# A two-layer hybrid mixer and expert kernel: the first layer's S5 matrices made ahead on GpSimd during SSD, queries stacked over 128 partitions, and parameter steps given a rank

## The chip, the cores and the metric

The kernel runs on one core of a Trainium2 chip. The metric is the device time of one execution in microseconds (us); smaller is better. Its engines are named as in the profile: PE (matrix products), PEld (its weight loads), DVE (VectorE), ACT (ScalarE), POOL (GpSimd), SP (the engine that issues most DMAs). Every engine runs its own instructions in the order in which they stand in its program; an instruction that waits holds up all behind it on that engine.

## What is computed

Two layers, each a token mixer and a mixture of experts, on 512 latent tokens and 256 context tokens of width 1024, in float32. Cut to what matters here:

```
h = modulate(rmsnorm(x), shift, scale)            # norm
proj = h @ w_in                                   # split into the branches' inputs
ya = softmax(q k^T) v        # attention: 8 query heads of 64, 2 key/value heads
yb = ssd_mixer(...)          # conv, then two directions of a chunked scan, 6 chunks of 128 tokens
yc = s5_mixer(u, lambda, step, B, C)  # 24 groups of 16 channels, 64 complex states, two directions
yd = bg * conv(cg * hh)      # gated short convolution
x  = x + g * ((sum of sigmoid(gate_i) * (y_i @ w_br_i)) @ w_out)     # merge
x  = x + g2 * expert_choice_ffn(...)              # 16 experts, gate/up/down of 1024 x 1024
```

S5 needs matrices that depend on the parameters alone and not on the tokens: powers of the complex step `exp(lambda*step)`, combined with B and C into blocks for eight tokens at a time. For each c of 0 to 5 (four groups) they are T (two parts of 128x384), B (two of 128x512, then transposed on PE), C (two of 128x640) and a block KK of products of B and C. A complex product (`cmul`) is six elementwise operations: four products, a difference and a sum.

## The kernel before

Layer 0's stages in the order of the time line, read from the trace (us from the span's start): norm to about 55; SSD 60 to 320, of which convolution and z to 170, states to 180 and the six chunks from 180; the S5 input projection 320 to 390 with the parameter preparation beside it; the S5 loop 390 to 560 and its output to 600; attention 600 to 840; the rest of the filler (below) 840 to 918; merge to 1120; the experts (MoE0) to 1795. Layer 1 repeats this without the context's outputs, up to 2600, and its experts end the program at 3126.

**Two kinds of work.** `ssd`, `s5` and `attention` are written out one after the other in `branches` with `filling` off; their weights go through the tiles `raw`, `cwH` and `cwL`. Then, with `filling` on, come `shortconv`, `gate` and the later columns of `mods`: the filler. It is independent of the branches, and a scheduler, which knows program order as priority, puts its matmuls (`psmm<-hH,fwH` and its two siblings, lines 99 to 101; `psmm<-fr,cpad`, L195, for `mods`) where it sees a gap on PE. Filler weights pass through three buffers each of `fr` (the raw 128x1024 block from DRAM), `fwH` and `fwL` (its two halves in the split precision), in the pool `st`. Gate results go to `tg` (two buffers). A product in the split precision takes three matmuls: high by high, low by high, high by low.

**SSD on the engines.** For each of six column blocks m, ACT copies the projection from PSUM to `xpad` (L662), DVE convolves, ACT takes the tanh, PE transposes, ACT copies. GpSimd clears the edges of `xpad` (L595), makes `xw` (L747, 10 of them), one of the two `S*E` products of a head pair (L811, 24) and adds the off-diagonal part to `y` (L827, 20).

**S5 matrices before.** In layer 0 they are made in the S5 loop itself, chunk c beside its use: GpSimd makes B and T (`Bx`, `Tr`: lines 990 to 995, called with `nc.gpsimd`), DVE makes C, PE transposes B (L1299) and forms KK (L1308). In layer 1 they are made ahead by the generator `s5_params`, one `next` per expert step in MoE0, on DVE, written to DRAM (`s5w`) from ACT's queue, and loaded in the loop into `mt`, 1664 KB for each c. In it one buffer, `s5T`, takes T of every c in turn, so that T of c+1 waits until c's has been written out.

**Attention before.** q and k are rotated in `R`; pairs of heads are transposed (L925) and split into `qTH`/`qTL`, with 64 partitions a head; each key head is doubled on DVE into `kd` before its transpose. `scores` forms q k^T with K=64 and the usual three matmuls for each head and each key half.

Of the kernel before, what the change touches and what calls it, by code (L numbers as in the profile page):

```python
# [45 lines left out]
_PS5 = {}  # L46
# [12 lines left out]
class Kern:  # L59
# [86 lines left out]
    def setup(self):  # L146
# [30 lines left out]
        self.s5w = {1: dr("s5w1", 6, 128, self.S5W)}  # L177
        self.s5r = {1: dr("s5r1", 128, 24)}
# [100 lines left out]
    def mixer(self, l):  # L279
# [42 lines left out]
    def norm(self, l):  # L322
        nc, L0 = self.nc, l == 0
        with self.pool("np") as np_:
# [24 lines left out]
            if L0:  # L349
                rows = []  # L350
                for q in range(5):
# [288 lines left out]
    def ssd(self):  # L640
# [12 lines left out]
        with self.pool("conv"):  # L653
            for m in (4, 5, 0, 1, 2, 3):
# [8 lines left out]
                self.vt = "a"  # L663
                cv = self.wp.tile([128, 770], F32, name="cv")
# [99 lines left out]
        with self.pool("core") as wp:  # L764
# [83 lines left out]
            for i, c in enumerate(self.tiles):  # L848
# [3 lines left out]
                y = chunk(c, *now)  # L852
                if last:
# [5 lines left out]
    def attention(self):  # L859
# [4 lines left out]
        qT = [wp.tile([128, 4, 768 - q0], F32R, name="qT" + p) for p in "HL"]  # L864
        kT = [wp.tile([128, 2, 768], F32R, name="kT" + p) for p in "HL"]
        Vt = wp.tile([128, NT, 128], F32, name="Vt")
        with self.pool("rope") as rp:
# [14 lines left out]
            for nm, m, c in (("k", 0, C_K), ("q", 0, C_Q), ("q", 1, C_Q + 256)):  # L882
# [31 lines left out]
                for o, n in (self.streams if nm == "q" else [(256, 512), (0, 256)]):  # L914
                    for g in range(2):
                        ps = self.va(n)
                        for i in range(n // 128):
                            t = o // 128 + i
                            if nm == "k":
                                kd = rp.tile([128, 2, 64], F32, name="kd", bufs=2)  # L920
                                V.tensor_copy(kd, R[:, t, g][:, None, :].to_broadcast([128, 2, 64]))
                                src = kd
                            else:
                                src = R[:, t, 2 * g:2 * g + 2]
                            nc.tensor.transpose(ps[:, i * 128:(i + 1) * 128], src.rearrange("p a c -> p (a c)"), self.ident)  # L925
                        self.split_to(*(z[:, 2 * m + g, o - q0:o - q0 + n] if nm == "q" else z[:, g, o:o + n] for z in (qT if nm == "q" else kT)), ps)
        R2 = [slice(0, 64), slice(64, 128)]

        def scores(t, hp):
# [8 lines left out]
            for i in range(np_):  # L938
                for hh in range(2):
                    q2, k2 = ([z[R2[hh], hp, tk] for z in qT], [z[R2[hh], hp // 2, i * pn:(i + 1) * pn] for z in kT])  # L940
                    self.mm3(sc[i][hh], [(*q2, *k2)])
# [57 lines left out]
    def s5_params(self, l, pool):  # L999
# [5 lines left out]
        sm = lambda nm, *s, tag=None: pool.tile([128, *(s or (24,))], F32, name="s5" + nm, tag="s5" + (tag or nm))  # L1005
        p5 = sm("p5", NPS5 - 384)
        Q.dma_start(p5, I["ps5"][l, :, 384:])
        pr = {k: p5[:, a - 384:b - 384] for k, (a, b) in _PS5.items()}

        step, mag, ang = sm("step"), sm("mag"), sm("ang")  # L1010
# [4 lines left out]
        t, sn, cn, rho = sm("t"), sm("sn"), sm("cn"), sm("rho")  # L1015
# [16 lines left out]
        x1 = sm("x1", 8, 24)  # L1032
# [12 lines left out]
        un, lo, hi = sm("un", 2, 9, 24), sm("lo", 2, 17, 24, tag="big"), sm("hi", 2, 6, 24)  # L1045
# [15 lines left out]
        for c in range(6):  # L1061
            gg = slice(4 * c, 4 * c + 4)
            T, e1 = sm("T", 2, 4, 6, 16, tag="out"), sm("e1", 4, 6, 16, tag="e1")
# [3 lines left out]
            Q.dma_start(out[c][:, 2560:], T.rearrange("p i g a b -> p (i g a b)"))  # L1067
            yield
        pw = sm("pw", 2, 9, 24, tag="un")
# [7 lines left out]
        nr, den, cr, ci = sm("nr"), sm("den"), sm("cr"), sm("ci")  # L1077
# [16 lines left out]
        PB, PC = sm("PB", 2, 8, 24), sm("PC", 2, 10, 24, tag="hi")  # L1094
# [8 lines left out]
        bb = [sm(f"bb{i}", 5, 16) for i in range(2)]  # L1103
# [3 lines left out]
        for c in range(6):  # L1107
# [4 lines left out]
            e1 = sm("e1", 4, 10, 16)  # L1112
            self.cmul(V, bb[0][:, :4], bb[1][:, :4], bc(cr), bc(ci), v3(pr["br"])[:, gg], v3(pr["bi"])[:, gg], e1[:, :, 0])
            Bx = sm("Bx", 2, 4, 8, 16, tag="big")
            ap = lambda P, n, i: P[:, i, :, gg].rearrange("p s g -> p g s")[:, :, :, None].to_broadcast([128, 4, n, 16])
            av = lambda v, n: v[:, :, None, :].to_broadcast([128, 4, n, 16])
            self.cmul(V, Bx[:, 0], Bx[:, 1], ap(PB, 8, 0), ap(PB, 8, 1), av(bb[0][:, :4], 8), av(bb[1][:, :4], 8), e1[:, :, :8])
            yield
            Bt = sm("Bt", 2, 4, 128, tag="out")
            for i in range(2):  # L1120
                ps = self.pa(512)
                for q in range(4):
                    nc.tensor.transpose(ps[:, q * 128:(q + 1) * 128], Bx[:, i, q].rearrange("p s i -> p (s i)"), self.ident)
# [3 lines left out]
            Cx = sm("Cx", 2, 4, 10, 16, tag="big")  # L1127
            self.cmul(V, Cx[:, 0], Cx[:, 1], ap(PC, 10, 0), ap(PC, 10, 1), av(cc[0][:, gg], 10), av(cc[1][:, gg], 10), e1)
            nc.scalar.mul(Cx[:, 1], Cx[:, 1], -1.0)
            for i in range(2):  # L1130
                Q.dma_start(out[c][:, 1024 + 512 * i:1536 + 512 * i].rearrange("p (g s j) -> p g (s j)", g=4, s=8),
                            Cx[:, i, :, 1:9].rearrange("p g s j -> p g (s j)"))
            yield

            KK = sm("KK", 4, 15, 16, tag="out")[:16]
            kf = [self.pa(128).rearrange("p (d j) -> p d j", d=8) for _ in range(2)]
            for d in range(2):
                r = slice(d * 64, d * 64 + 64)
# [12 lines left out]
            yield  # L1151

    def s5(self):
# [20 lines left out]
        hoisted = l == 1  # L1174
        if hoisted:
            s5d, rho = wp.tile([128, 384], F32, name="s5d"), wp.tile([128, 24], F32, name="rho")
            nc.scalar.dma_start(s5d, self.I["ps5"][l, :, :384])
            nc.scalar.dma_start(rho, self.s5r[l])
        else:
            keep = lambda nm, *s: wp.tile([128, *s], F32, name=nm)  # L1180
            bb = [keep("bbr", 25, 16), keep("bbi", 25, 16)]
            cc = keep("cc", 2, 24, 16)
            s5d = keep("s5d", 384)
            PB, PC = keep("PB", 2, 8, 24), keep("PC", 2, 10, 24)
            rho = keep("rho", 24)
            lo, hi = keep("lo", 2, 17, 24), keep("hi", 2, 6, 24)
            with self.pool("s5p") as pp:
                sm = lambda nm, *s: pp.tile([128, *(s or (24,))], F32, name=nm)
                p5 = sm("p5", NPS5 - 384)
                nc.scalar.dma_start(p5, self.I["ps5"][l, :, 384:])  # L1190
                nc.scalar.dma_start(s5d, self.I["ps5"][l, :, :384])
                pr = {k: p5[:, a - 384:b - 384] for k, (a, b) in _PS5.items()}
                V.tensor_copy(cc[:, 0], v3(pr["cr"]))
                V.tensor_copy(cc[:, 1], v3(pr["ci"]))

                step, mag, ang = sm("step"), sm("mag"), sm("ang")
                nc.scalar.activation(step, pr["ls"], AF.Exp)
                V.tensor_mul(mag, pr["lr"], step)
                nc.scalar.activation(mag, mag, AF.Exp)
                V.tensor_mul(ang, pr["li"], step)  # L1200
                t, sn, cn = sm("t"), sm("sn"), sm("cn")
                M = 12582912.0
                V.tensor_scalar(t, ang, 1.0 / (2 * np.pi), M, op0=OP.mult, op1=OP.add)
                V.tensor_scalar(t, t, M, None, op0=OP.subtract)
                V.scalar_tensor_tensor(ang, t, -6.28125, ang, op0=OP.mult, op1=OP.add)
                V.scalar_tensor_tensor(ang, t, -(2 * np.pi - 6.28125), ang, op0=OP.mult, op1=OP.add)
                V.tensor_scalar(ang, ang, 3.1415925, -3.1415925, op0=OP.min, op1=OP.max)
                nc.scalar.activation(sn, ang, AF.Sin)
                nc.scalar.activation(cn, ang, AF.Sin, scale=0.5)
                V.tensor_mul(cn, cn, cn)  # L1210
                V.tensor_scalar(cn, cn, -2.0, 1.0, op0=OP.mult, op1=OP.add)
                pw = sm("pw", 2, 9, 24)
                x1 = sm("x1", 8, 24)
                V.memset(pw[:, 0, 0], 1.0)
                V.memset(pw[:, 1, 0], 0.0)
                V.tensor_mul(pw[:, 0, 1], mag, cn)
                V.tensor_mul(pw[:, 1, 1], mag, sn)

# [587 lines left out]
```

## Time and profile before

| | |
|---|---|
| median of 3 runs | 3125.06 us (3124.32 to 3130.27) |
| the profiled execution | 3127.88 us, span 3126.0 us, mean granted clock 0.970 |
| PE busy in the span | 2857.1 us (91%) |
| DVE / ACT / POOL busy | 1615.0 (52%) / 790.0 (25%) / 444.5 (14%) us |
| layer 0 before its merge | 0 to 918 us |
| the S5 loop of layer 0, of layer 1 | 390 to 560, 2095 to 2200 us |
| layer 1's experts | 2600 to 3126 us, DMA at 409 GB/s |

The shares of the whole span hide that each stage has its own limit. PE is busy nearly all the time in layer 0 but for the first 40 us and for the S5 loop; in layer 1's experts the weights' transfer sets the pace. A view by stretch (busy time of each engine in windows) therefore tells more here than the page's totals. In that view "PEclk" is the granted clock of TensorE as a share of its upper level: 1.00 is 2.4 GHz, 0.50 would be 1.2 GHz, and values between are means over a stretch. Matmuls are pipelined, so that the mean duration of one is longer than the distance between two starts.

### The profile page before, as it was taken

How to read it: one execution, taken by the hardware profiler on the slowest of the kernel's cores; microseconds unless marked ns; L12 is line 12 of the kernel's file. 1: busy time of each engine (PE TensorE's matmuls, PEld its weight loads, DVE VectorE, ACT ScalarE, POOL GpSimd, SP SyncE). 2: the span in 40 equal slices, each digit the busy share in tenths (PEclk: the TensorE clock that was granted, in tenths of full speed). 3: DMA queues.
4: the chain of work that ended last, by engine and by line, in shares of the span. 5: the costliest groups of instructions: out<-in, count | busy, mean ns of one | idle time of the engine just before them, and what ended most of it. 6: DMA issues, size and time to landing. Idle time of an engine off the chain costs nothing. (4 is left out here: it accounts for less than half of the span.)

```text
span 3126.0 us, 47474 instructions
## 1 busy us (share of the span) xinstructions
PE 2857.1 (91%) x18866; PEld 1850.2 (59%) x18866; DVE 1615.0 (52%) x3681; ACT 790.0 (25%) x1733; POOL 444.5 (14%) x551
## 2 busy tenths in 40 slices
PE   7999878999999976999999979999999996998887
PEld 4866756787788952444444448577777884332223
DVE  5477688655326676354522264767654365232223
ACT  4253222425422210011100033321445221000001
POOL 1022265100004120000010010400000031010001
PEclk9999989999999988999999989999999998999999
DMA  7324424311247357898998663255312576999997
GB/s 234 114 67 132 141 86 126 121 48 35 98 156 226 123 204 290 346 344 330 352 372 332 235 210 98 63 167 199 98 44 80 199 265 256 409 409 409 409 409 301
DMA packets 328832, 667.18 MB, mean 213 GB/s; under 512 B 22177, under 2 KB 197537, under 8 KB 327842
## 3 DMA queue, kind: packets, MB, share of 16 engines
q1 hardware_dynamic: 297712, 610.31, 54.4%
q10 hardware_dynamic: 27378, 43.18, 3.8%
q0 software_dynamic: 3520, 10.65, 0.9%
q8 instruction: 149, 2.44, 0.3%
q14 instruction: 73, 0.60, 0.1%
HBM read 609.94 MB, written 52.56 MB: 212 GB/s over the span
## 5 line engine op out<-in xcount | busy, mean ns | idle before, releaser
L1507 PE MATMUL psa<-we,X 128*64 128x512 f32 (+1 forms) x4096 | 593.2, 492 | 49.1 <-DMA we<-in_w_exp_gate_dram 18.3
L1507 PEld LDWEIGHTS psa<-we,X 128*64 128x64 f32 (+1 forms) x4096 | 202.5, 124 | 406.3 <-issue 279.1
L99 PE MATMUL psmm<-hH,fwH 128*128 128x512 f32 x984 | 369.9, 376 | 6.8 <-DVE xpad L632 3.6
L101 PE MATMUL psmm<-hH,fwL 128*128 128x512 f32 x984 | 365.1, 371 | 0.0
L100 PE MATMUL psmm<-hL,fwH 128*128 128x512 f32 x984 | 363.9, 370 | 0.0
L1539 PE MATMUL psa<-we,hidT 128*64 128x512 f32 x992 | 243.9, 611 | 16.1 <-ACT hidT L1527 11.1
L99 PEld LDWEIGHTS psmm<-hH,fwH 128*128 128x128 f32 x984 | 188.1, 191 | 51.7 <-issue 15.3
L101 PEld LDWEIGHTS psmm<-hH,fwL 128*128 128x128 f32 x984 | 188.1, 191 | 33.0 <-issue 6.7
L100 PEld LDWEIGHTS psmm<-hL,fwH 128*128 128x128 f32 x984 | 188.3, 191 | 31.5 <-issue 6.3
L1520 ACT ACTIVATE hid<-psa 128x512 f32<-128x512 f32 (+1 forms) x48 | 25.3, 527 | 605.4 <-PE psa L1507 442.7
L115 DVE TENSOR_TENSOR fwL<-fr,fwH 128x1024 fp32r<-128x1024 f32 (+1 forms) x100 | 109.6, 1097 | 124.0 <-ACT fwH L114 113.4
L1539 PEld LDWEIGHTS psa<-we,hidT 128*64 128x64 f32 x992 | 70.9, 139 | 159.4 <-issue 121.3
L1544 DVE SCALAR_TENSOR_TENSOR y<-psa,ag,m 64x512 f32<-64x512 f32 x62 | 46.5, 749 | 224.6 <-PE psa L1539 223.9
L1498 POOL TENSOR_TENSOR X<-X,modT 128x512 f32<-128x512 f32 x40 | 41.5, 1050 | 697.2 <-DVE X L1497 694.5
L469 POOL TENSOR_TENSOR merged<-merged,tgm 128x512 f32<-128x512 f32 (+1 forms) x48 | 62.5, 1321 | 516.8 <-DMA y<-ys 274.4
L99 PE MATMUL psa<-cwH,hH 128*128 128x256 f32 (+1 forms) x432 | 122.4, 284 | 1.7 <-DVE dtv L697 1.6
L114 ACT CAST fwH<-fr 128x1024 fp32r<-128x1024 f32 (+1 forms) x100 | 89.4, 895 | 132.2 <-PE psmm L100 70.0
L101 PE MATMUL psa<-cwH,hL 128*128 128x256 f32 (+1 forms) x432 | 121.6, 282 | 0.0
L100 PE MATMUL psa<-cwL,hH 128*128 128x256 f32 (+1 forms) x432 | 121.4, 281 | 0.0
L1522 DVE TENSOR_TENSOR hid<-hid,psa 128x512 f32<-128x512 f32 (+1 forms) x48 | 28.7, 597 | 176.7 <-PE psa L1507 176.4
L1521 DVE SCALAR_TENSOR_TENSOR hid<-hid,psa 128x512 f32<-128x512 f32 (+1 forms) x48 | 28.7, 598 | 144.4 <-ACT hid L1520 144.3
L414 ACT ACTIVATE tg<-psmm 128x512 f32<-128x512 f32 x96 | 50.9, 530 | 202.1 <-PE psmm L101 202.0
(645 smaller groups left out, 5860.6 us busy)
## 6 DMA issues: line engine op xcount, KB each, us to landing
we<-in_w_exp_gate_dram SPq DMA_DIRECT2D x128, 1024.0 KB, 8.7
we<-in_w_exp_up_dram SPq DMA_DIRECT2D x128, 1024.0 KB, 13.8
we<-in_w_exp_down_dram SPq DMA_DIRECT2D x128, 1024.0 KB, 15.1
fr<-in_w_mod_dram SPq DMA_DIRECT2D x96, 512.0 KB, 6.5
fr<-in_w_in_dram SPq DMA_DIRECT2D x64, 512.0 KB, 4.2
raw<-in_w_in_dram SPq DMA_DIRECT2D x36, 512.0 KB, 4.0
gs<-tg ACTq DMA_DIRECT2D x32, 384.0 KB, 2.8
tgm<-gs SPq DMA_DIRECT2D x32, 384.0 KB, 3.3
```

Source lines behind the costliest of these rows:

```text
L99: self.nc.tensor.matmul(ps, ah, bh, start=start and i == 0, stop=False)
L100: self.nc.tensor.matmul(ps, ah, bl, start=False, stop=False)
L101: self.nc.tensor.matmul(ps, al, bh, start=False, stop=stop and i == n - 1)
L114: self.nc.scalar.copy(h, x)
L115: self.nc.vector.tensor_sub(l, x, h.bitcast(F32))
L414: nc.scalar.activation(tg[:, o:o + n], self.cm(w, m, o, n), AF.Tanh, scale=0.5)
L469: (V if i == 3 else nc.gpsimd).tensor_add(dst, dst, t)
L1498: nc.gpsimd.tensor_add(X[:, hk], X[:, hk], Bm[:, 24 + h * 4:28 + h * 4, s:s + 1].to_broadcast([128, 4, 128]))
L1507: self.lastup = nc.tensor.matmul(ps[s][j * c:(j + 1) * c], X[s][:, k, r:r + c], w(k)[:, j * n:(j + 1) * n], start=k == 0, stop=k == 7, ski ...
L1521: V.scalar_tensor_tensor(hid, hid, 1.0, g, op0=OP.add, op1=OP.mult)
L1539: nc.tensor.matmul(ps[j * c:(j + 1) * c], lh, w(k)[:, j * n:(j + 1) * n], start=k == 0, stop=k == 7, skip_group_check=True)
L1544: V.scalar_tensor_tensor(Y[s][r, nn], ps[j * c:(j + 1) * c], got[s][1][r, e:e + 1], m5[s][r, nn], op0=OP.mult, op1=OP.mult)
```

## The change

Three things are changed.

1. **Layer 0's S5 matrices are made ahead.** `s5_params(0, st)` starts before the norm, and `advance()` takes one step of it at places in the norm, the convolution, z, the states and the chunks of SSD, with its priority number raised by 600 (a later rank). What is left is drained before `s5`. All six operations of each big product of T, B and C are on GpSimd (`E`), the small ones on DVE. Results go to DRAM and come back into `mt` as in layer 1. Its scratch tiles take all three buffers of each of `fwH`, `fwL` and `fr`, and one of `tg`; C and B share the places `c0` and `c1`, and T, the transposed B and KK share `out`.
2. **Rank in MoE0.** Layer 1's steps go through `advance` too, and from expert 1 on.
3. **Queries stacked.** Each query head is doubled into `kd`, now on GpSimd with three buffers, and transposed alone; `qS` holds the high part on partitions 0 to 63 and the low part on 64 to 127. A score is then two matmuls with K=128 (`qS` by `kTH`, `qS` by `kTL`).

```diff
                 with self.psum(*MIX[l]):
+                    if l == 0:
+                        self.ahead = self.s5_params(0, st)
+                        next(self.ahead)
                     self.norm(l)
@@ norm, in the loop over q
+                    if q > 2:
+                        self.advance()
@@ branches
+            if nm == "s5":
+                for _ in self.ahead:
+                    pass
@@ ssd: convolution, z, states, chunks
                 self.vt = "a"
+                self.advance()
...
             for t in range(NT):
+                self.advance()
...
                 for i, c in enumerate(order[:-1]):
+                    self.advance()
...
                 y = chunk(c, *now)
+                for _ in range(2):
+                    self.advance()
@@ attention
-        qT = [wp.tile([128, 4, 768 - q0], F32R, name="qT" + p) for p in "HL"]
+        qS = wp.tile([128, 8, 768 - q0], F32R, name="qS")
...
+                            kd = rp.tile([128, 2, 64], F32, name="kd", bufs=3)
+                            nc.gpsimd.tensor_copy(kd, R[:, o // 128 + i, g][:, None, :].to_broadcast([128, 2, 64]))
+                            nc.tensor.transpose(ps[:, i * 128:(i + 1) * 128], kd.rearrange("p a c -> p (a c)"), self.ident)
...
+                            z = qS[:, 4 * m + g, o - q0:o - q0 + n]
+                            nc.scalar.copy(z, ps)
+                            V.tensor_sub(z[64:], ps[64:], z[64:].bitcast(F32))
...
-                    self.mm3(sc[i][hh], [(*q2, *k2)])
+                    for z in range(2):
+                        nc.tensor.matmul(sc[i][hh], qS[:, 2 * hp + hh, tk], kT[z][:, hp // 2, i * pn:(i + 1) * pn], start=z == 0, stop=z == 1)
@@ s5_params
+        E = V if l else nc.gpsimd
...
+            for i, nm in enumerate(("pa", "c0", "c1", "e1", "hi", "un", "PB", "sm", "out")):
+                tag = ("fwH", "fwL", "fr")[i // 3]
+                place[nm] = pool.tile([128, 1024], F32, name="s5" + nm, tag=tag, bufs=3)
...
-            self.cmul(V, T[:, 0], T[:, 1], h4(0), h4(1), l4(0), l4(1), e1)
+            self.cmul(E, T[0], T[1], h4(0), h4(1), l4(0), l4(1), e1)
...
+    def advance(self):
+
+        p = self.tc.cur_priority
+        self.tc.cur_priority = p + 600
+        next(self.ahead, None)
+        self.tc.cur_priority = p
@@ s5: the branch that made the matrices in the loop is gone
-                    self.cmul(nc.gpsimd, Bx[0], Bx[1], ap(PB, 8, 0), ap(PB, 8, 1), av(bb[0], 8), av(bb[1], 8), e1)
-                    self.cmul(V, Cx[0], Cx[1], ap(PC, 10, 0), ap(PC, 10, 1), av(cc[:, 0], 10), av(cc[:, 1], 10), z1)
...
-                    self.cmul(nc.gpsimd, T[0], T[1], h4(0), h4(1), l4(0), l4(1), e1[:, :, :6])
+                mt = bp.tile([128, self.S5W], F32, name="mt", bufs=2)
+                nc.sync.dma_start(mt, self.s5w[l][g0 // 4])
@@ experts, after each k
-                    if k == 1:
-                        next(self.ahead, None)
+                    if k == 1 and e:
+                        self.advance()
```

How the instructions stand, in the order of each engine's program (out<-in by tile names; xN: N alike in a row).

PE before, in the convolution of SSD, where the first filler matmul stands (the 130th row of PE's program):

```order
L100 MATMUL psb<-hL,cwH 128x256
L101 MATMUL psb<-hH,cwL 128x256
L99 MATMUL psmm<-hH,fwH 128x512
L100 MATMUL psmm<-hL,fwH 128x512
L101 MATMUL psmm<-hH,fwL 128x512
```

PE of the change, the place of the first filler matmul (the 788th row); L853 transposes y of SSD's last chunk, L1164 transposes B, L1182 is KK:

```order
L1182 MATMUL psb<-s5c_125,s5sm 32x128
L853 MATMUL psa<-cst,y 128x128 x4
L1164 MATMUL psb<-cst,s5c_124 128x128 x4
L1164 MATMUL psb<-cst,s5c_125 128x128 x4
L1182 MATMUL psb<-s5c_124,s5sm 32x128
L99 MATMUL psmm<-hH,fwH 128x512
```

No filler matmul stands between SSD's instructions any more; the steps of `s5_params` do.

POOL before, from the end of the norm into SSD:

```order
L347 TENSOR_TENSOR hL<-hf,hH 128x512
L347 TENSOR_TENSOR hL<-hf,hH 128x256
L595 MEMSET xpad 128x1 x28
L747 TENSOR_TENSOR xw<-x_tok,wdd 128x512 x10
L811 TENSOR_TENSOR S<-S,E 128x128 x4
```

POOL of the change, at the end of the norm (lines 1004 to 1009 are one complex product, here T; L350 is the norm's last `hL`, L603 the edges of `xpad`):

```order
L1009 TENSOR_TENSOR s5out<-s5out,s5e_126 128x384
L1005 TENSOR_TENSOR s5e_126<-s5hi,s5c_124 128x384
L350 TENSOR_TENSOR hL<-hf,hH 128x512
L350 TENSOR_TENSOR hL<-hf,hH 128x256
L1004 TENSOR_TENSOR s5out<-s5hi,s5c_124 128x384
L350 TENSOR_TENSOR hL<-hf,hH 128x512
L350 TENSOR_TENSOR hL<-hf,hH 128x256
L1006 TENSOR_TENSOR s5out<-s5out,s5e_126 128x384
L603 MEMSET xpad 128x1 x4
```

Thirteen T operations stand before the norm's fifth pair of `hL` and fourteen before the sixth; all 36 and B and C of c=0 to 2 stand before the last `xw`, c=3 and 4 among the chunks' `S*E` and `y`, and c=5 behind them.

ACT before, in the convolution:

```order
L662 COPY xpad<-psa 128x512
L114 CAST cwH<-raw 128x1056
L114 CAST cwH<-raw 128x4x256
L662 COPY xpad<-psa 128x256
L198 COPY row<-psmm 128x256
L667 ACTIVATE th<-cv 128x770
```

ACT of the change, in front of the copy of m=2 (L1165 copies the transposed B, L1170 negates a part of C, L1186 and L1188 copy KK, L1166, L1172 and L1190 issue writes to `s5w`):

```order
L1186 COPY s5out<-psb 16x128 x4
L1188 COPY s5out<-psb 16x112
L695 COPY x_tok<-psa 128x4x128
L695 COPY x_tok<-psa 128x2x128
L1188 COPY s5out<-psb 16x112 x3
L1190 DMA s5w_91<-s5out 16x4x128 x6
L670 COPY xpad<-psa 128x512
```

KK of c=0 stands before `xpad` of m=2, KK of c=1 before z, KK of c=2 before the first decays of the chunks. In MoE0 the order on DVE is that of before at the place where T of layer 1 is made: these operations stand between the two halves of expert 1's `hid`.

## Rows read from the trace of the kernel before

**Rows 1.** Busy time by stretch, all engines, layer 0's stages and layer 1's S5 loop.

```profile
core 0: us, PE busy (x) PEld busy (x) DVE busy (x) ACT busy (x) POOL busy (x), PEclk, DMA share, GB/s
60.00:180.00 120.00, 117.82 (x785) 98.38 (x783) 57.27 (x109) 34.13 (x63) 11.00 (x30) 1.00 0.34 99
180.00:320.00 140.00, 131.72 (x751) 93.93 (x752) 104.46 (x290) 72.55 (x204) 33.26 (x49) 1.00 0.36 109
320.00:390.00 70.00, 63.04 (x408) 51.00 (x412) 46.05 (x169) 18.12 (x31) 15.39 (x14) 0.95 0.43 138
390.00:560.00 170.00, 143.19 (x1137) 108.84 (x1124) 146.00 (x244) 43.21 (x103) 97.39 (x89) 0.89 0.34 103
560.00:918.00 358.00, 348.93 (x2369) 284.11 (x2367) 161.05 (x459) 145.52 (x361) 16.25 (x16) 0.99 0.25 81
2095.00:2200.00 105.00, 98.18 (x625) 74.28 (x624) 80.87 (x192) 21.96 (x31) 9.52 (x25) 0.98 0.50 168
```

**Rows 2.** The same for tile fwH: columns PE, PEld, DVE, ACT, clock, DMA.

```profile
60.00:320.00 260.00, 91.34 (x332) 56.09 (x333) 14.24 (x18) 12.41 (x18) 1.00 0.35 104
840.00:880.00 40.00, 36.38 (x150) 25.51 (x151) 7.35 (x6) 6.30 (x6) 1.00 0.61 212
```

**Rows 3.** The same for tile fwL: PE, PEld, DVE, clock, DMA.

```profile
60.00:320.00 260.00, 57.75 (x166) 31.28 (x166) 14.24 (x18) 1.00 0.35 104
840.00:880.00 40.00, 25.28 (x76) 14.30 (x76) 7.35 (x6) 1.00 0.61 212
```

**Rows 4.** The same for line L195 (mods) in SSD: PE, PEld, clock, DMA.

```profile
60.00:320.00 260.00, 14.18 (x160) 4.60 (x160) 1.00 0.35 104
```

**Rows 5.** The same for lines L1308 (KK), then L1299 (B transposed), around the loop.

```profile
300.00:620.00 320.00, 7.97 (x192) 4.28 (x192) 0.93 0.40 124
...
300.00:620.00 320.00, 6.44 (x48) 5.45 (x48) 0.93 0.40 124
```

**Rows 6.** Time line of POOL, norm: start, duration, instruction, idle before.

```profile
38.46 2.89 POOL L347 TENSOR_TENSOR hL<-hf,hH 128x512 fp32r<-128x512 f32 x2 [2.78 <-DVE hf L346]
...
52.23 1.97 POOL L347 TENSOR_TENSOR hL<-hf,hH 128x512 fp32r<-128x512 f32 x2 [1.35 <-DVE hf L346]
```

**Rows 7.** Busy time by stretch, tile Tr (DVE, POOL), then tile Bx (PE, PEld, POOL).

```profile
300.00:620.00 320.00, 25.13 (x48) 33.99 (x24) 0.93 0.40 124
...
300.00:620.00 320.00, 6.44 (x48) 5.45 (x48) 35.03 (x24) 0.93 0.40 124
```

**Rows 8.** POOL operations on tile e: duration ns min/median/max.

```profile
L991 POOL TENSOR_TENSOR e<-PB,bbi x6: 1102/1372/1584, 362.5 to 511.0; 128x512 f32<-128x512 f32 x6
```

**Rows 9.** Tile s5T in MoE0: operation, then idle before it and who waited.

```profile
L990 DVE TENSOR_TENSOR s5T<-s5hi,s5lo x6: 1108/1116/1118, 1170.6 to 1226.1; 128x384 f32<-128x384 f32 x6
...
  DMA s5w<-s5T: 18.6, 5
...
  ACT hid L1520: 35.7, 1
```

**Rows 10.** DMA issues of the page: tile, queue, count, KB, median us to landing.

```profile
s5w<-s5Cx ACTq DMA_DIRECT2D x12, 256.0 KB, 12.9
```

**Rows 11.** Groups of POOL operations up to 620 us: busy us, mean ns, idle before.

```profile
L827 POOL TENSOR_TENSOR y<-y,yo 128x256 f32<-128x256 f32 x20 | 18.7, 937 | 23.7 <-DVE y L816 10.2 <-DVE rs_y L126 4.8 <-DVE rs_t L125 3.0
L811 POOL TENSOR_TENSOR S<-S,E 128x128 f32<-128x128 f32 x24 | 13.5, 561 | 61.4 <-DVE S L810 59.5 <-PE psmm L101 1.2 <-DVE rs_y L136 0.6
L747 POOL TENSOR_TENSOR xw<-x_tok,wdd 128x512 f32<-128x512 f32 x10 | 11.1, 1149 | 55.4 <-DVE wdd L738 55.4
```

**Rows 12.** Time line of DVE in MoE0: one of the small parameter operations.

```profile
1170.02 0.18 DVE L991 TENSOR_TENSOR s5x<-s5hi 128x24 f32<-128x24 f32 x1
```

**Rows 13.** Time line of PE in layer 1's attention: two transposes, three score matmuls.

```profile
2286.78 0.38 PE L925 MATMUL psa<-cst,R 128*128 128x128 f32 x2
2287.09 0.44 PE L99 MATMUL psa<-kTH,qTH 64*128 64x384 f32 x1
...
2287.81 0.50 PE L101 MATMUL psmm<-hH,fwL 128*128 128x512 f32 x1
```

**Rows 14.** Groups of POOL operations in the whole span that have one input.

```profile
L1468 POOL COPY pick<-identb 16x128 bf16<-16x128 bf16 x20 | 6.2, 321 | 121.3 <-PE psmm L1470 119.7 <-PE psmm L101 1.6
```

**Rows 15.** POOL in the whole span: two-input additions of 128x128 in attention.

```profile
L908 POOL TENSOR_TENSOR R<-R,tp 128x128 f32<-128x128 f32 x4 | 2.8, 706 | 32.7 <-DVE tp L907 30.0 <-DVE rs_v L124 2.7
```

More of the change, by code (lines that the diff above doesn't have):

```diff
@@ L175, in setup @@
         self.gs = [dr(f"gs{b}", 8, 128, 768) for b in range(4)]
-        self.s5w = {1: dr("s5w1", 6, 128, self.S5W)}
-        self.s5r = {1: dr("s5r1", 128, 24)}
+        self.s5w = [dr(f"s5w{l}", 6, 128, self.S5W) for l in range(2)]
+        self.s5r = [dr(f"s5r{l}", 128, 24) for l in range(2)]
         self.hr = [[dr(f"hr{l}{s}", n, D) for s, n in enumerate((512, 256)[:2 - l])] for l in range(2)]
@@ L1004, in s5_params, with at, small, bank @@
         v3 = lambda a: a.rearrange("p (g i) -> p g i", g=24)
[L1005 to L1010, printed above, removed]
+        E = V if l else nc.gpsimd
+        place = {}
+        if l:
+            for nm, n in (("pa", 840), ("pb", 768), ("c0", 816), ("c1", 640), ("out", 1024), ("e1", 640), ("hi", 480), ("un", 432), ("PB", 384), ("sm", 616)):
+                place[nm] = pool.tile([128, n], F32, name="s5" + nm)
+        else:
+            for i, nm in enumerate(("pa", "c0", "c1", "e1", "hi", "un", "PB", "sm", "out")):
+                tag = ("fwH", "fwL", "fr")[i // 3]
+                place[nm] = pool.tile([128, 1024], F32, name="s5" + nm, tag=tag, bufs=3)
+            place["pb"] = pool.tile([128, 768], F32, name="s5pb", tag="tg", bufs=2)
+        used = [0]
+        def at(nm, *shape, o=0):
+            n = int(np.prod(shape))
+            ax = "abcd"[:len(shape)]
+            return place[nm][:, o:o + n].rearrange(f"p ({' '.join(ax)}) -> p {' '.join(ax)}", **dict(zip(ax, shape)))
+        def small(*shape):
+            shape = shape or (24,)
+            used[0] += int(np.prod(shape))
+            return at("sm", *shape, o=used[0] - int(np.prod(shape)))
+        def bank(n):
+            return self.pa(n) if l else self.va(n, "b")
+        pr = {}
+        for nm, o, n in (("pa", 384, 840), ("pb", 1224, 768)):
+            Q.dma_start(place[nm][:, :n], I["ps5"][l, :, o:o + n])
+            pr.update({k: place[nm][:, c - o:d - o] for k, (c, d) in _PS5.items() if o <= c < o + n})
+        step, mag, ang = (small() for _ in range(3))
         nc.scalar.activation(step, pr["ls"], AF.Exp)
@@ L1014, in s5_params @@
         V.tensor_mul(ang, pr["li"], step)
-        t, sn, cn, rho = sm("t"), sm("sn"), sm("cn"), sm("rho")
+        t, sn, cn, rho = (small() for _ in range(4))
         M = 12582912.0
@@ L1031, in s5_params @@
         yield
-        x1 = sm("x1", 8, 24)
+        x1 = small(8, 24)
         def powers(P, first, last):
@@ L1062, in s5_params @@
             gg = slice(4 * c, 4 * c + 4)
-            T, e1 = sm("T", 2, 4, 6, 16, tag="out"), sm("e1", 4, 6, 16, tag="e1")
+            T, e1 = [at("out", 4, 6, 16, o=i * 384) for i in range(2)], at("e1", 4, 6, 16)
             h4 = lambda i: hi[:, i, :, gg].rearrange("p a g -> p g a")[:, :, :, None].to_broadcast([128, 4, 6, 16])
             l4 = lambda i: lo[:, i, 1:17, gg].rearrange("p a g -> p g a")[:, :, None, :].to_broadcast([128, 4, 6, 16])
-            self.cmul(V, T[:, 0], T[:, 1], h4(0), h4(1), l4(0), l4(1), e1)
-            Q.dma_start(out[c][:, 2560:], T.rearrange("p i g a b -> p (i g a b)"))
+            self.cmul(E, T[0], T[1], h4(0), h4(1), l4(0), l4(1), e1)
+            Q.dma_start(out[c][:, 2560:], place["out"][:, :768])
             yield
-        pw = sm("pw", 2, 9, 24, tag="un")
+        pw = at("un", 2, 9, 24)
         V.memset(pw[:, 0, 0], 1.0)
@@ L1075, in s5_params @@
         yield
-        nr, den, cr, ci = sm("nr"), sm("den"), sm("cr"), sm("ci")
+        nr, den, cr, ci = (small() for _ in range(4))
         ni = pw[:, 1, 1]
@@ L1102, in s5_params @@
         yield
-        bb = [sm(f"bb{i}", 5, 16) for i in range(2)]
+        bb = [small(5, 16) for i in range(2)]
         for b in bb:
@@ new lines, in s5 @@
+                mt = bp.tile([128, self.S5W], F32, name="mt", bufs=2)
+                nc.sync.dma_start(mt, self.s5w[l][g0 // 4])
+                Bt = [mt[:, i * 512:i * 512 + 512].rearrange("p (q c) -> p q c", q=4) for i in range(2)]
+                Cx = [mt[:, 1024 + i * 512:1536 + i * 512].rearrange("p (q c) -> p q c", q=4) for i in range(2)]
+                T0 = mt[:, 2048:2560].rearrange("p (q c) -> p q c", q=4)
+                T = [mt[:, 2560 + i * 384:2944 + i * 384].rearrange("p (q c) -> p q c", q=4) for i in range(2)]
@@ L1341, in s5 @@
                 H = [W(f"Vr{i}", 4, 96) for i in range(2)]
[L1342 removed]
+                g1, g2 = W("g1", 4, 96), W("g2", 4, 96)
                 V.tensor_mul(H[0], T[0], pv[0])
```

189 lines of the change are left out of this document (25 added, 164 removed).

## The prediction

> **What bounds the kernel now.** I read the busy time by stretch first, since a change to one stage is worth what that stage's limit lets through; then what the filler takes in SSD, POOL's operations in the norm and the S5 loop, the waits around T in MoE0, and one stretch of attention.
>
> From 60 to 320 us PE is busy 117.82 + 131.72 of 260 us at clock 1.00 [rows 1]: SSD has no gap to speak of, because filler lies in its gaps. How much: fwH's matmuls are busy 91.34 us there and fwL's 57.75 [rows 2, 3], together 149.1; these overlap, and in 840 to 880, where there is little else, 36.38 + 25.28 = 61.7 us of them fill 40 us [rows 2, 3]. So the filler takes 149.1 x 40/61.7 = 97 us of PE in SSD; the mods matmuls another 14.18 busy [rows 4], about 10 by the same ratio. SSD's own PE work is 249.5 - 107 = 142.5 us.
>
> In the S5 loop PE is busy 143.19 of 170 us at a clock of 0.89, with DVE at 146 and POOL at 97 [rows 1]. At full clock its work is 143.19 x 0.89 = 127 us: 43 us is lost to waiting and to the clock. Layer 1's loop, with its matrices loaded, is busy 98.18 of 105 us at 0.98 [rows 1], a loss of 9. That difference is what the first part can win there. Attention is bound by PE: 348.93 of 358 us from 560 to 918 [rows 1].
>
> **Layer 0 as a sum.** Once the filler may start, PE has work to the end of the layer: whatever is left is done one after the other. So the end of the stage before the merge is T + W + L: T the time at which the filler starts, W PE's work that is left, L what is still lost. Before, it is 918.
>
> W: the work from 60 to 918 at full clock is 249.5 + 63.04 x 0.95 + 143.19 x 0.89 + 348.93 x 0.99 = 782 us [rows 1]. SSD's own 142.5 goes off, and the 8 + 6 us of KK and B transposes [rows 5], which now lie ahead of T. That leaves 625. Attention's saving takes 14 off (below): W = 611. L: 9 in the S5 loop as in layer 1, 13 elsewhere (358 - 345 from 560 on): 22. The end is T + 633, plus 4 for `kd` (below). Layer 0 breaks even at T = 281.
>
> **T, the price.** Filler weights need the buffers in which the parameters' scratch lies, and in PE's order the first filler matmul comes behind the last KK; so T is the end of the GpSimd chain of 36 operations each for T, B and C, or the end of SSD, whichever is later. The T part of the generator has a lower end and an upper end:
>
> - An operation with `Tr` as its output took 33.99/24 = 1.42 us on POOL, one with `Bx` 35.03/24 = 1.46 [rows 7]; the e products are alike. So T takes 8.5 us for a c, B 8.8, and C, with 640 for 512 elements, 10.9 (worked out from B). The fastest product of 512 took 1.10 [rows 8]: then 6.6, 6.6 and 8.3. In all 169 us, or 129.
> - T's single output buffer: in MoE0 the next T sat behind the write 18.6 us in 5 times, 3.7 us each [rows 9]. B of c+1 overwrites what C of c lies in, which ACT must negate, PE read and a DMA write; such a write landed in 12.9 us in MoE0 [rows 10], whose DMA load was higher than SSD's 0.34 to 0.36 [rows 1]. I take 5, near the lower row, and 1.2 for eight B transposes at 0.155 [rows 13].
> - The first T can start when four pairs of `hL` are done, 38.46 + 2.89, about 42 [rows 6]. Two more pairs (2 us each) lie within: the T part ends at 42 + 51 + 5 x 3.7 + 4 = 115. Each c then takes 8.8 + 10.9 + 1.2 + 5 = 25.9, six 155: 270. SSD's own POOL work, 18.7 + 13.5 + 11.1 = 43 us [rows 11], lies in between, half of it in the waits: 292, and 296 with the last KK.
> - ACT's order ties SSD to the chain: KK of c=0 stands in front of `xpad` for m=2, KK of c=2 in front of the chunks' decays. KK of c=2 is there at 115 + 3 x 25.9 = 193, with `xw` on POOL 204. The six chunks took 140 us with filler, and DVE is busy 104 of these [rows 1], some of it for filler; without, I take 104: T = 308.
>
> T = 308, then, from two ways that agree within 12 us. The end of the stage is 308 + 633 + 4 = 945, 27 us later than 918. The floor: the T part ends at 42 + 40 + 18.5 = 101 with `hL` in its waits, a c takes 6.6 + 8.3 + 1.2 + 3.7 = 19.8, KK of c=2 is there at 160, `xw` at 171, and the chunks take 100, without the filler's share of DVE (of 14.24 in SSD [rows 2]): T = 271. The ceiling: 12.9 in the place of 5 gives 33.8 for a c, KK of c=2 at 216, 227 with `xw`, chunks 104 to 140: 331 to 367.
>
> The norm: 60 small DVE operations of 0.18 us [rows 12] now stand ahead of the reciprocal root, at most 11 us, and T operations ahead of the last two `hL` pairs, which ended at 54 [rows 6]. Both delay SSD's begin; it costs nothing in the sum above, since the chain on GpSimd is later anyway, and up to 11 where it is not. PE will wait in SSD, and its granted clock will sink as it did in the S5 loop (0.89). That costs nothing while GpSimd is last; were it PE, 157 us at 0.89 would be 19 more.
>
> The Trainium skill (GPSIMD Engine Reference, Elementwise — side-by-side cycle accounting) puts a two-input float32 operation on GpSimd at 1.96 times VectorE's. The same product of 128x384 took 1.116 on DVE [rows 9], which would make 2.19 on GpSimd; POOL's rows say 1.42 on the mean [rows 7]. The measurement decides; by the page's ratio T's 24 products would take 24 x 0.77 = 18 us more, and the forecast would be 3161.
>
> **Attention.** In layer 1's attention three score matmuls took from 2287.09 to 2287.81, 0.72 us [rows 13], for two now 0.48: 0.24 less. Layer 0 has 4 tiles x 8 heads x 2 halves = 64 of 384 columns and 16 of 256, 15.4 + 2.6 us; layer 1 64, 15.4. Transposes: 24 more in layer 0, 16 in layer 1, at most 0.155 each [rows 13]: 3.7 and 2.5. So 14 and 13 us less on PE. Against it, `kd` comes from GpSimd, 60 copies and 44, in bursts between which PE has one filler matmul for three transposes. With 226 filler matmuls in 40 us [rows 2, 3] that is (3 x 0.155 + 0.18)/3 = 0.215 us for each transpose. A one-input copy of 128 elements took 0.321 on POOL, though of 16 partitions [rows 14]; a two-input addition of 128x128 0.706 [rows 15]. I take 0.32: PE loses 0.1 for some 39 and 35 transposes that are not first in a burst, 4 us in each layer. By 0.706 it would be 19 and 17, by none 0. The Trainium skill (GPSIMD Engine Reference, Engine selection) says that one-input operations run at about line rate on GpSimd; by it the 8 us would be near nothing. Layer 1 gains 13 - 4 = 9, on the path, since PE is the limit there.
>
> **Rank.** T of layer 1 still stands between the halves of expert 1's `hid`, behind which ACT waited 35.7 us [rows 9]. The order there is that of before, so I cost it at nothing; were those waits gone, 18.6 us of DVE's waiting would be the gain.
>
> **The sum.** 3127.9 + 27 - 9 = 3146 by the profiled execution, which is 2.8 above the median of the runs: 3143.
>
> **The rivals.**
>
> *SSD runs freely without the filler.* PE is no longer shared and the chain runs at POOL's fastest rows: T = 271, 37 us less, 3106. For it: 107 us of foreign work leaves SSD, and DVE is less loaded than beside POOL in the S5 loop (146 of 170). Against it: KK of c=2 must then be there by 160, with no SSD work of POOL in its way. It turns to a gain where T is below 290.
>
> *The single buffers decide.* Writes land in 12.9 us: T = 331, 3166, and up to 3202 with slow chunks. For it: B and C share their places, T, B and KK another, and ACT must issue eleven writes for a c in between its own SSD work. Against it: DMA is loaded a third only.
>
> *`kd` on GpSimd holds PE.* At 0.706 the gain of attention is eaten in both layers: 28 us more, 3171 with T = 308, 3134 with T = 271.
>
> *The rank ends the wait in MoE0.* 3124 with the rest as forecast, no change. The order speaks against it.
>
> **The numbers.** My forecast's own region (T from 296 to 330) has a chance of 0.42, 3131 to 3165. The free SSD 0.27; the buffers or `kd`, above that, 0.20; what lies about break-even, the rank among it, 0.11. No change is within 0.2%, about 6 us, T from 284 to 296. So faster 0.27, same 0.11, slower 0.62. The range for 8 in 10 goes from 3102, below the free SSD, to 3182, between the buffers' two prices.
>
> **What would show it.** Right: by stretch, PE well under full from 60 to 300 with POOL busy, and the first `psmm<-hH,fwH` at about 308; POOL's T operations from 42 to 115; ACT's `xpad` waiting for KK; the S5 loop near 105 us; merge starting at about 945; fewer PE us in attention, PE waiting there for POOL `kd` in pieces of a tenth of a us. Wrong: the first filler before 280, the chunks' first decays before 190, or a c on POOL of 20 us or less. Then the free SSD is what happened. A start after 330 with POOL idle for the writes would be the buffers.

## The result, and the profile after

The changed kernel takes 3295.14 us (median; 3293.98 to 3299.1) against 3127.07 for before on the same chip: a ratio of 1.0547, 95% interval 1.0523 to 1.0571. It is slower by 168 us. The prediction had the sign and not the size: it gave 3143, with a range up to 3182.

The page of the changed kernel: span, busy time and share by engine, and the granted clock in 40 slices.

```profile
span 3293.0 us, 47471 instructions
PE 2907.8 (88%) x18762; PEld 1882.2 (57%) x18762; DVE 1597.6 (49%) x3661; ACT 797.7 (24%) x1745; POOL 515.4 (16%) x691
PEclk9685599999999998899899998999999998899999
```

The clock sinks in slices 2 to 5, about 80 to 410 us: that is SSD. Where else time went is read from instructions that both kernels have. In both traces, tile by tile, columns count: duration ns min/median/max, first to last start; here the experts' first matmul, and the first step of a norm on `x`, layer 1's begin. Before:

```profile
L1507 PE MATMUL psa<-we,X x4096: 379/498/1114, 1143.6 to 3094.3; 128*64 128x512 f32 x99, 128*32 128x256 f32 x97
...
L333 ACT ACTIVATE junk<-x x6: 1052/1053/1057, 1807.2 to 1819.7; 128x1024 f32<-128x1024 f32 x6
```

The changed kernel:

```profile
L1417 PE MATMUL psa<-we,X x4096: 379/498/1117, 1278.9 to 3261.1; 128*64 128x512 f32 x99, 128*32 128x256 f32 x97
...
L336 ACT ACTIVATE junk<-x x6: 1052/1054/1057, 1985.8 to 1999.0; 128x1024 f32<-128x1024 f32 x6
```

Layer 0's mixer is 135 us longer (1278.9 - 1143.6), MoE0 another 43 (1985.8 - 1807.2 is 179), and layer 1 gives 12 back (167 at the end).

By stretch in the changed kernel (columns as in [rows 1]): SSD in three parts, and layer 0's S5 loop.

```profile
80.00:200.00 120.00, 68.67 (x424) 58.62 (x423) 44.66 (x71) 25.63 (x54) 66.02 (x63) 0.74 0.22 63
200.00:240.00 40.00, 30.52 (x236) 24.57 (x236) 22.46 (x49) 9.63 (x19) 16.76 (x14) 0.83 0.33 99
240.00:400.00 160.00, 99.23 (x336) 61.35 (x334) 105.33 (x262) 69.01 (x207) 74.72 (x79) 0.54 0.13 37
440.00:545.00 105.00, 97.84 (x782) 76.57 (x781) 85.25 (x201) 14.70 (x29) 11.70 (x38) 1.00 0.62 203
```

The loop gave what layer 1's showed: 105 us in the place of 170 [rows 1]. SSD lost more. PE has less to do there than before, is busy for 62% of the time from 240 to 400 us, at a granted clock of 0.54, and the filler starts only at 401 us:

```profile
L99 PE MATMUL psmm<-hH,fwH x984: 276/393/793, 401.1 to 2636.5; 128*128 128x512 f32 x131, 128*128 128x256 f32 x66
```

So T, forecast at 308, is 401. The waits say what SSD stood in. First PE's from 60 to 235 us, then POOL's from 60 to 407 (engine, line, what it waited for: us in all, times, longest); L691 transposes the convolution's output, L1182 is KK, L1164 the transposes of B, L1004 the first operation of C.

```profile
PE psa L691 <- DVE cv L684: 21.8, 2, 19.7
PE psb L1182 <- POOL s5c L1006: 14.2, 3, 5.3
PE psb L1164 <- POOL s5c L1006: 11.6, 2, 9.8
PE psb L1182 <- ACT s5c L1170: 7.5, 2, 3.8
...
POOL s5c L1004 <- PE psb L1164: 44.8, 3, 35.3
```

PE waits at KK and at the transposes for GpSimd (14.2 and 11.6 us, and 7.5 more for the part of C that ACT negates), with SSD's matmuls behind them. Its wait for `cv` is in sum no longer than without any S5 steps, where it is 24.8 us (the held run below). From 235 to 407 PE waits another 22 us at the same two places. GpSimd in turn waits for PE's transposes, which stand behind SSD's matmuls in PE's order. The longest of these waits on POOL's time line (idle before it in brackets), and all engines in that stretch:

```profile
221.29 1.57 POOL L1004 TENSOR_TENSOR s5c<-s5hi,s5pb 128x640 f32<-128x640 f32 x1 [35.33 <-PE psb L1164]
...
185.96:221.30 35.34, 35.30 (x297) 35.13 (x296) 14.12 (x44) 8.66 (x18) 0.01 (x2) 1.00 0.24 70
```

Here GpSimd stood for 35 us in front of C, for eight transposes that were sized at 1.2 us. PE did not wait in that time: it was busy for 35.30 of 35.34 us at clock 1.00, nearly all of it with SSD's own z projection. So this wait held back the S5 chain and not SSD, and the steps behind it came to lie among the chunks.

### The profile page after: what moved, and what is told of

Same layout as the page of the kernel before. It is cut to its first block, busy times and chain, and to the rows that moved or that the text cites. A ratio compares the mean times of both kernels' runs of the same rounds, so it can differ in the third digit from the quotient of the medians.

```text
span 3293.0 us, 47471 instructions
## 1 busy us (share of the span) xinstructions
PE 2907.8 (88%) x18762; PEld 1882.2 (57%) x18762; DVE 1597.6 (49%) x3661; ACT 797.7 (24%) x1745; POOL 515.4 (16%) x691
## 5 line engine op out<-in xcount | busy, mean ns | idle before, releaser
L1417 PE MATMUL psa<-we,X 128*64 128x512 f32 (+1 forms) x4096 | 610.9, 497 | 44.6 <-DMA we<-in_w_exp_gate_dram 16.3
```

The lines of the kernel that those rows point to most:

```text
L1417: self.lastup = nc.tensor.matmul(ps[s][j * c:(j + 1) * c], X[s][:, k, r:r + c], w(k)[:, j * n:(j + 1) * n], start=k == 0, stop=k == 7, ski ...
```

## The experiments

Theory: three separate causes. Layer 0's mixer is long because the filler is shut out of SSD and because S5 steps stand in line with SSD's instructions; MoE0 is long because of the rank; attention gains. Rivals are in each expectation. Each time of the kernel before was taken on the same chip as the run beside it.

**Rank undone** (in the changed kernel):

```diff
-                    if k == 1 and e:
-                        self.advance()
+                    if k == 1:
+                        next(self.ahead, None)
```

> The changed kernel with one part undone: in MoE0 layer 1's parameter steps are taken as before, from expert 0 on and without the later rank. In the changed kernel the time line stands 134 us behind before at MoE0's begin and 179 behind at its end. Theory 1 (the rank costs these 44 us, because it spreads the steps into experts where PE has nothing else to hide them): 3295 - 44 = about 3251. Theory 2 (the new layout of the scratch, in which whole places are shared, makes the steps wait): no change, 3295 within 6.

Measured: 3241.09 us (3239.94 to 3245.71), 54 less than the changed kernel. The rank, not the scratch's layout, is MoE0's loss.

**Attention alone** (the kernel before with the new `qS`, `scores` and `kd`):

> The kernel before with the attention of the change alone: stacked queries, two score matmuls, kd on GpSimd. Theory 1 (PE is the limit in both layers, kd costs little): 14 - 4 and 13 - 4 us less, 3127 - 19 = about 3108. Theory 2 (kd on GpSimd holds PE): 3127 within 6. In the changed kernel layer 1 gained 12 us between the ends of MoE0 and of its merge, which speaks for theory 1.

Measured: 3107.7 against 3124.07, a ratio of 0.9944 (0.9928 to 0.9961): 16 us, near theory 1. Its experts' first matmul, and the `kd` copies in the changed kernel (0.343 us each on the mean):

```profile
L1508 PE MATMUL psa<-we,X x4096: 378/498/1116, 1133.1 to 3075.1; 128*64 128x512 f32 x99, 128*32 128x256 f32 x97
...
L933 POOL COPY kd<-R 128x128 f32<-128x128 f32 x60 | 18.4, 343 | 19.6 <-DVE R L927 12.1 <-PE psa L934 7.3
```

**No parameter work in layer 0:**

```diff
-                        self.ahead = self.s5_params(0, st)
-                        next(self.ahead)
+                        for c in range(6):
+                            nc.sync.dma_start(self.s5w[0][c], I["w_in"][0, c * 128:c * 128 + 128, :self.S5W])
+                        nc.scalar.dma_start(self.s5r[0], I["w_in"][0, 0:128, 4000:4024])
```

> The changed kernel without any parameter work in layer 0: its S5 matrices are not made, the DRAM blocks that the loop loads are filled from w_in by seven transfers at the start. The filler's buffers are then free in SSD. It leaves out the making of layer 0's S5 matrices, and says what the hoist is worth at no price. Theory 1 (all that the hoist costs lies in SSD, and the S5 loop gives back what layer 1's loop shows): layer 0 gains 43 - 9 = 34 in the loop and 10 in attention, layer 1 gains 10, the rank costs 44: 3127 - 54 + 44 = about 3117. Theory 2 (PE has no less to do, and the idle time only moves): 3127 - 20 + 44 = about 3151.

Measured: 3122.49 against 3124.07 (ratio 0.9998, 0.9989 to 1.0008), 5 above theory 1. But its seven transfers stand ahead of the norm's loads: the convolution's first tanh starts at 94.2 us in the place of 60.3 (below), 34 us later. Where layer 0's mixer ends is read from the experts' first matmul, before the rank has any part:

```profile
L1418 PE MATMUL psa<-we,X x4096: 378/498/1117, 1108.4 to 3092.8; 128*64 128x512 f32 x99, 128*32 128x256 f32 x97
```

It comes 35 us earlier than before (1143.6) in spite of the 34; attention alone gives 10.5 of that (1133.1). So making the S5 matrices ahead, at no price, is worth about 35 + 34 - 10.5 = 59 us, more than the 34 of theory 1.

**The same with the filler's buffers held** through SSD:

```diff
+                        self.hold = [st.tile([128, 1024], F32, name=f"hold{i}", tag=("fwH", "fwL", "fr")[i // 3], bufs=3) for i in range(9)]
+                        for h in self.hold:
+                            nc.gpsimd.memset(h[:, :1], 0.0)
...
+                for h in self.hold:
+                    nc.vector.tensor_add(h[:, :1], h[:, :1], last[1][:, :1])
```

> As the run without parameter work, but nine tiles hold all buffers of fr, fwH and fwL from the norm until the last chunk of SSD is finished, so that the filler starts where it does in the changed kernel. It leaves out the making of layer 0's S5 matrices. Theory 1 (SSD was slow because its engines stood in line behind the S5 steps): SSD ends at about 300 instead of 401, and the time is about 3295 - 100 = 3195. Theory 2 (SSD is slow because PE, without filler, falls to the lower clock): SSD ends at 370 or later with a granted clock of 0.5 to 0.6 in the chunks, and the time is 3265 or more.

Measured: 3231.25 us (two runs), between the two theories. Against the run without parameter work that is 109 us for nothing but the filler's absence from SSD. Its experts' first matmul, and PE's wait for `cv` in SSD:

```profile
L1422 PE MATMUL psa<-we,X x4096: 379/498/1117, 1212.5 to 3201.5; 128*64 128x512 f32 x99, 128*32 128x256 f32 x97
...
PE psa L693 <- DVE cv L686: 24.8, 4, 7.0
```

Filler begins at 347 us. SSD as such, from the first tanh to the last copy `yT`, is read from the next rows: one group each of before, the changed kernel, no parameter work, and held. The last `xw`, shown for two of them, stands where the chunks begin.

```profile
L667 ACT ACTIVATE th<-cv x6: 845/852/855, 60.3 to 127.3; 128x770 f32<-128x770 f32 x6
...
L844 ACT COPY yT<-psa x6: 586/587/589, 224.8 to 317.8; 128x512 f32<-128x512 f32 x6
```

```profile
L676 ACT ACTIVATE th<-cv x6: 845/847/851, 76.6 to 177.6; 128x770 f32<-128x770 f32 x6
...
L758 POOL TENSOR_TENSOR xw<-x_tok,wdd x10: 1042/1042/1224, 225.9 to 240.2; 128x512 f32<-128x512 f32 x10
...
L855 ACT COPY yT<-psa x6: 586/586/587, 296.5 to 406.1; 128x512 f32<-128x512 f32 x6
```

```profile
L677 ACT ACTIVATE th<-cv x6: 845/851/852, 94.2 to 161.1; 128x770 f32<-128x770 f32 x6
...
L856 ACT COPY yT<-psa x6: 585/587/587, 256.9 to 350.2; 128x512 f32<-128x512 f32 x6
```

```profile
L678 ACT ACTIVATE th<-cv x6: 845/846/852, 90.9 to 162.3; 128x770 f32<-128x770 f32 x6
...
L760 POOL TENSOR_TENSOR xw<-x_tok,wdd x10: 1037/1218/1222, 204.3 to 214.2; 128x512 f32<-128x512 f32 x10
...
L857 ACT COPY yT<-psa x6: 585/585/586, 257.4 to 344.4; 128x512 f32<-128x512 f32 x6
```

SSD takes 257.5 us before, 256.0 with filler and no parameter work, 253.5 with neither, and 329.5 in the changed kernel. To take out its 97 us of filler (the prediction's estimate) makes SSD 2.5 us shorter. The S5 steps make it 76 longer: 30 in the convolution (first to last tanh 101.0 for 71.4) and 46 behind it.

**Held, with matmuls that nothing reads:**

```diff
+        if self.l == 0 and not self.filling:
+            ps = self.pa(512)
+            for i in range(12):
+                self.nc.tensor.matmul(ps, self.hH[:, i % 8, :128], self.hH[:, i % 8, :512], start=i == 0, stop=i == 11)
```

> As the run with held buffers, with matmuls added that nothing reads: twelve of 128x512 at each of the places in SSD where the change takes a parameter step, of the later rank, about 100 us of PE work in all, as much as the filler took there before. It leaves out the making of layer 0's S5 matrices. In the held run the granted clock is 0.50 to 0.60 in the chunks, and SSD takes 267 us from its first tanh to the last chunk's end, no less than before with the filler. Theory 1 (an emptier PE runs at the lower clock, and that eats what the filler's leaving gives): the clock stays at 0.9 to 1.0, and SSD takes 235 us or less although PE has 100 us more to do. Theory 2 (SSD's own chain over PE, ACT and DVE has that length): 262 us or more.

Measured: 3238.18 us. The chunks by stretch, held first, then with the added matmuls, and the latter's SSD:

```profile
240.00:340.00 100.00, 63.06 (x181) 40.38 (x180) 62.27 (x185) 40.04 (x117) 24.20 (x38) 0.53 0.09 27
```

```profile
240.00:330.00 90.00, 83.50 (x371) 59.77 (x370) 58.50 (x175) 31.92 (x95) 21.52 (x34) 0.96 0.10 30
...
L676 ACT ACTIVATE th<-cv x6: 851/852/853, 91.3 to 156.2; 128x770 f32<-128x770 f32 x6
...
L758 POOL TENSOR_TENSOR xw<-x_tok,wdd x10: 1037/1218/1224, 197.0 to 206.9; 128x512 f32<-128x512 f32 x10
...
L855 ACT COPY yT<-psa x6: 585/587/587, 246.8 to 331.2; 128x512 f32<-128x512 f32 x6
```

By the ends shown SSD takes 239.9 us, 13.6 less than held, although 374 of the 480 added matmuls, 106 us of busy time, lie in it. (The 267 us that the expectation names for held ran on into the S5 projection; by these ends it is 253.5, and both thresholds are 13 too high.) Both theories hold in part: the lower clock costs 14 us, and the rest, 240, stays although PE is near the upper level. How long SSD would be with an empty PE at the full clock no run shows. Against these added matmuls the filler itself is not free: with it SSD takes 256.0 at clock 1.00, 16 more than here. Its cost and the clock's worth happen to be nearly equal. The gain does not show in the time, since the last of the added matmuls ran at 385.5 and the filler started behind them, at 398.5.

**Layer 0's products on VectorE:**

```diff
-        E = V if l else nc.gpsimd
+        E = V
```

> The changed kernel with layer 0's 108 big operations on VectorE in place of GpSimd, still in SSD and in the filler's buffers, rank as changed. Theory 1 (GpSimd's operations, 169 us in one order with SSD's own, are what SSD waits for): DVE does the products in 1.1 us and the sums in 0.55, some 60 us less for the chain, and SSD ends 30 us or more before 401. Theory 2 (the chain waits for its single buffers and for ACT, and DVE is SSD's own busiest engine): SSD ends at 390 or later, the time is 3285 or more.

Measured: 3263.22 us, a ratio of 1.0452 to before where the changed kernel has 1.0547: about 30 us less. The filler starts at 370.7, 30 earlier.

```profile
L676 ACT ACTIVATE th<-cv x6: 842/847/853, 73.4 to 151.3; 128x770 f32<-128x770 f32 x6
...
L855 ACT COPY yT<-psa x6: 586/586/586, 259.0 to 359.1; 128x512 f32<-128x512 f32 x6
```

SSD takes 285.7: of the 76 us that the S5 steps add, 44 go when DVE makes the products in GpSimd's place, and 32 stay. Of the 44, 30 reach the filler: the last S5 steps now stand behind SSD's end and in front of it. This is theory 1, but GpSimd is not the whole of the cause.

**`kd` on VectorE** (attention alone as above, `V.tensor_copy` for `nc.gpsimd.tensor_copy`):

> The kernel before with the stacked queries, but kd made on VectorE as before. With kd on GpSimd the run took 3107.7 us, 16 less than before, where PE's work is 27 less. Theory 1 (kd on GpSimd holds PE up, 4 us in a layer by a copy of 0.34 us): with 0.22 us on VectorE some 6 less, about 3102. Theory 2 (the copies are covered by filler wherever they are made): 3108 within 3.

Measured: 3099.2 against 3122.46, a ratio of 0.9924 (0.9896 to 0.9951). That is 8.5 less than with `kd` on GpSimd, but on another chip, and the intervals of the two ratios overlap, so the times alone do not tell them apart. PE's waits for `kd` do differ, in layer 0 and layer 1, first on GpSimd, then on VectorE:

```profile
PE psa L921 <- POOL kd L920: 3.7, 4, 1.6
...
PE psa L921 <- POOL kd L920: 3.0, 3, 1.3
```

```profile
PE psa L921 <- DVE kd L920: 1.4, 3, 0.7
...
PE psa L921 <- DVE kd L920: 1.0, 2, 0.5
```

That is 6.7 against 2.4 us: theory 1 by the waits, with 4 us shown in them and the rest open.

**The rank in two halves,** on that base. First the later rank alone, then leaving out expert 0 alone:

```diff
                     if k == 1:
+                        p = tc.cur_priority
+                        tc.cur_priority = p + 600
                         next(self.ahead, None)
+                        tc.cur_priority = p
```

> The kernel before with stacked queries and kd on VectorE (3099.2 us), and one thing of the change more: layer 1's parameter steps in MoE0 are issued with the later rank of 600, from expert 0 on. The changed kernel lost 54 us to its way of issuing these steps. Theory 1 (the rank itself costs it: steps drift into later experts, where PE waits for them): 3140 to 3155. Theory 2 (leaving out expert 0 costs it): 3099 within 8.

```diff
-                    if k == 1:
+                    if k == 1 and e:
```

> The same base (3099.2 us) with the other half of it: no later rank, but no step at expert 0. Theory 1 (the rank itself costs the 54 us): 3099 within 8. Theory 2 (leaving out expert 0 costs it, because the last steps then come later): 3140 to 3155.

Measured: 3146.44 with the rank (ratio 1.0071, 1.0053 to 1.0089), 3091.93 without expert 0 (0.9915, 0.9892 to 0.9938). The rank costs 47 to 54 us; leaving out expert 0 costs nothing. PE's waits in MoE0 with the rank, at KK and at B's transposes:

```profile
PE psmm L1142 <- DVE s5Cx L993: 18.1, 6, 5.2
PE psmm L1124 <- DVE s5Bx L993: 7.8, 1, 7.8
```

and the base's largest wait there:

```profile
PE psb L1526 <- DVE hid L1523: 8.0, 3, 5.8
```

With the rank PE waits 26 us inside the experts for parameter products that DVE has not made; the base has no such wait. All of MoE0 by stretch, with the rank and then the base:

```profile
1127.70:1839.80 712.10, 648.96 (x5203) 266.62 (x5203) 299.97 (x634) 71.62 (x160) 49.43 (x56) 0.95 0.79 300
```

```profile
1126.50:1796.40 669.90, 629.97 (x5203) 262.08 (x5203) 295.44 (x633) 71.61 (x161) 48.64 (x56) 0.97 0.84 319
```

It is 42 us longer in these two traces: PE is idle for 23 us more, and busy for 19 us more with the same 5203 matmuls, at a granted clock of 0.95 in the place of 0.97. Why PE comes to these steps before DVE has made their products was not tried.

## Why the prediction was right or wrong

- **T, the price: wrong, and the step that failed.** It had 308 us; 401 was measured. The work was sized well: T's products ended at 106 (115 forecast), from

```profile
L1009 POOL TENSOR_TENSOR s5out<-s5out,s5e x6: 992/1001/1877, 53.8 to 104.6; 128x384 f32<-128x384 f32 x6
```

  S5's 108 operations kept POOL busy for 150 us (169), and a one-input copy took 0.343 (0.32). Two terms of the sum failed. The first is the 1.2 us "for eight B transposes": POOL waited 44.8 us for those of c=0 to 2, since in PE's order they stand behind SSD's matmuls, and the last `xw` ended at 241, not 204. The second is the chunks: I took 104 us, DVE's busy time, for the length of a stage in which the engines wait for each other. From 241 to the filler's start it was 160. From the last `xw` to the last `yT` held takes 130 without any S5 steps, and with the added matmuls, near the upper clock, 124: so of the 56 us too few some 20 are SSD's own chain, 6 the clock and 30 the S5 steps. I let each engine's chain run beside the others, with the other engines' answers at the price of their work. They are in one order on each engine: the S5 steps make SSD 76 us longer, and 44 of these go when DVE makes the products. The norm adds 16 (76.6 for 60.3), where I allowed up to 11 and counted nothing; what in it makes the 16 was not tried. Nor does the first filler matmul come behind the whole of the last KK, as I read from the order: 30 of its 32 matmuls ran later, up to 414.6.
- **SSD without filler: no gain to be had.** The whole of SSD is 253.5 us with neither filler nor S5 steps, about as long as before. The rival "SSD runs freely" is refuted by the held run alone: its filler starts at 347, and even without the 31 us by which its SSD began later that is 316, behind the 290 below which it would gain.
- **The clock: wrong to cost it at nothing.** It sank to 0.54 from 240 to 400 us, not to the S5 loop's 0.89, and is worth 14 us in the held run.
- **Layer 0 as a sum: nearly right.** With the measured T it gives 401 + 637 = 1038, 120 us later; the stage came 135 later. Formed as in the prediction (busy time by stretch times clock), PE's work behind T was 625 where W had 611, and the loss 28 where L and `kd` had 26: the 15 us lie in W.
- **The S5 loop: right in the trace** (105 us) and in the sum. At no price the prediction's own terms give the first part of the change 34 us in the loop, 14 for KK and the transposes, and 10 that PE lost from 320 to 390 (70 - 63.04 x 0.95), for which L has nothing: 58, and about 59 were measured. The 34 in the expectation of that run left out the other two.
- **Attention: right.** 19 us forecast, 16 measured alone. Of the 8 for `kd` on GpSimd, PE's waits show 6.7, though in seven pieces of up to 1.6 us and not in many of a tenth.
- **Rank: wrong, the other failed step.** I costed it at nothing because the order at T's place in MoE0 was that of before. That was one place of many: with the rank alone layer 1's B was first written at 1360.0 in the place of 1310.0 and the last of KK at 1677.8 in the place of 1546.1, PE waited 26 us for these products, and the rank costs 47 to 54 us.
- **The buffers' rival: not what happened.** The write of T held POOL 5.5 us in all, and after 330 POOL was not idle for writes.

Together, by the experts' first matmul (before 1143.6, attention alone 1133.1, no parameter work 1108.4, held 1212.5, changed 1278.9) and SSD's begin in each: 10 gained in attention and 59 by making the matrices ahead at no price; lost 107 by the filler's absence, 81 by the S5 steps (76 of them inside SSD) and 16 in the norm. That makes the 135 us of layer 0's mixer. These are differences along one chain of runs, so that they add up by themselves: the sum checks nothing, and the 59 is what is left over. With MoE0's 43 and layer 1's 12 it is the 167 us between the two traces.

The kernel before with stacked queries and `kd` on VectorE, with or without the step at expert 0, is faster than both kernels: 3099.2 and 3091.93 us; the two are not told apart.

## What to carry to other kernels

Before a stage gives up its filler, ask what sets its length: where it is a chain over engines, filler in it may cost little (here the clock that it kept up gave back 14 of 16 us), and to take it out brings next to nothing while all of it must be paid later. An engine's busy time is not the length of such a stage. Work that hops between engines can cost the queue in front of each hop, and not its own duration; count the hops and what stands in line there. And where an order is read as evidence for "unchanged", read it through to the last of the moved instructions.

## What the runs showed that was not expected

PE busy for 63 of 100 us had a granted clock of 0.53, near the lower level of 1.2 GHz; with matmuls that nothing reads, 83.5 of 90 us, it had 0.96, and the whole of SSD was 14 us shorter. Seven transfers of 10 MB in all, put ahead of the norm's loads, moved the begin of layer 0's SSD by 31 to 34 us.
